# Last feed-forward, first octo: its first product looks two weight tiles ahead instead of four

## The chip, the core and the metric

The kernel runs on one core of a Trainium2 chip. The core has five engines with instruction streams of their own, each worked off in order: TensorE (PE; PEld is its weight load), VectorE (DVE), ScalarE (ACT), GpSimd (POOL) and SyncE (SP), which here only starts transfers. Engines wait for each other on semaphores alone. The metric is the device time of one execution in microseconds (us); lower is better. Times inside a profile count from the start of its span.

## The reference

One layer of a decoder on 512 tokens of width 1024, in float32: a half-step SwiGLU feed-forward, a token mixer (a gated linear recurrence beside sliding-window attention), and a second half-step SwiGLU feed-forward. Each has an RMS norm ahead of it and one behind it. The change lies in the second feed-forward:

```python
def rms_norm(x, g):
    xf = x.astype(jnp.float32)
    y = xf * lax.rsqrt(jnp.mean(xf * xf, axis=-1, keepdims=True) + RMS_EPS)
    return (y * g.astype(jnp.float32)).astype(x.dtype)

def swiglu(x, w_gu, w_down):
    gate, up = jnp.split(x @ w_gu, 2, axis=-1)
    return (jax.nn.silu(gate) * up) @ w_down

    x = x + 0.5 * rms_norm(swiglu(rms_norm(x, ffn2_pre_g[l]), ffn2_w_gu[l], ffn2_w_down[l]), ffn2_post_g[l])
```

The hidden width is 2816, 22 chunks of 128.

## The kernel before

**Split products.** Each float32 operand is split into a rounded high part and the rest. ACT casts the high part (`whi` for weights, `hh` for hidden values), DVE subtracts it to get the low part (`wlo`, `hl`). A product is three matmuls on PE: high by high, high by low, low by high. So each weight tile costs one ACT cast and one DVE subtraction before PE can use it, and PE needs the low part at its second or third matmul.

**Groups of the last feed-forward.** The 22 chunks go in groups (0,6), (6,10), (10,14), (14,18), (18,22). The first group is computed chunk by chunk; its two first chunks go down at once (`classic_down`, results in `yb`). Each of the four others is an "octo": gate and up of four chunks by seven block products instead of eight (method `octo`, L929). Behind each octo come the seven products of the group before it on its way down (`seven_down`, L1083; banks `ya`, `yb`, `yd`, `ye`). The octo with the change is the one of chunks 6 to 9, here "octo 6".

**The seven products of an octo.** Their accumulators are three pairs of PSUM banks, A, D and B (`ab`, `db`, `bb` in the profile). In order: p into A; ACT copies A to B (L953, `each(act.copy, B, A)` at L979); q into D; ACT copies D away; r onto A; s onto B; t onto A; u onto D; v onto A. PE may not start r before the copies of A to B are done, since r goes on accumulating in A.

**The weight tiles of an octo.** Each product uses two weight units, one per half of 512 rows; the profile names them by product and number, such as `whi_bq__6333` and `wlo_bq__6334` for the first q unit and `whi_bq__6337`, `wlo_bq__6338` for the second. Gate and up blocks lie in four raw tiles loaded by SP: `raw_bx__6015`, `raw_bx__6121` (upper rows) and `raw_by__6243`, `raw_by__6246` (lower rows). Some units need a combination of blocks first, made on DVE in place (L294, "pre"): for q and s from the x tile alone, for r from the x tile and the y tile of the same number. Then come the cast on ACT (L283) and the subtraction on DVE (L287).

**What sets the order.** A planner, the class `Weights`, records these instructions when a product takes its unit. `take(ahead)` brings the units up to `ahead` behind the one taken into the streams. While `early` holds, it also rounds one unit more (its pre and its cast) before the low part of the unit at hand. `early` holds when `ahead` is at least `AHEAD`, which is 4:

```python
            if self.rounded == self.split:
                self.round()
            if early and self.rounded == self.split + 1 < len(self.units) and self.units[self.rounded][4]:
                self.round()
            ...
            if early and self.rounded == self.split:
                self.round()
...
        self.fill(1 + ahead, early or ahead >= AHEAD)
```

Whatever is recorded later stands later in its engine's stream. The copies of A to B are recorded behind the two takes of product p and ahead of the takes of product q. There are six buffers each for `whi` and `wlo`, and five for raw tiles.

**Beside the products** the octo also carries the forms for the way down: DVE makes sums of hidden values (`s1` to `s4`), ACT casts them (`hhs`, L824), DVE takes the low parts (`hls`, L831). The fifth product on the way down (bank `ye`) needs the low part of `s4`.

Of the kernel before, what the change touches and what calls it, by code (L numbers as in the profile page):

```python
# [21 lines left out]
FC = F // P  # L22
# [14 lines left out]
AHEAD = 4  # L37
# [84 lines left out]
def tile_layer(ctx: ExitStack, tc: tile.TileContext, out: bass.AP, **ins: bass.AP):  # L122
# [29 lines left out]
    def acc_tile(name):  # L152
        return tmp.tile([P, T], F32, tag="acc", name=name, bufs=3)

    def r_tile(name):
        return big.tile([P, T], F32, tag="R", name=name)

    def wide(name):
        return big.tile([P, NB * T], F32, tag="z", name=name, bufs=2)
# [5 lines left out]
    W = Weights()  # L165
# [630 lines left out]
    class Hidden:  # L796
# [129 lines left out]
            for j in range(2):  # L926
                self.hs[f + j] = hs[j]

        def octo(self, f, beside, soon=False):  # L929


            n = f"{self.name}{f}"

            def did(i):
                for fn in beside.get(i, ()):
                    fn()

            h_hbm = hbm.tile([4 * P, T], F32, name=f"h_{n}")

            def seven(b, form, first, i):  # L940
                for q in range(2):
                    hi, lo = W.take(3 if soon and i == 6 and q else AHEAD)
                    for tb in range(2):
                        blk = slice(tb * P, (tb + 1) * P)
                        for k in range(2):
                            xh, xl = self.nxt.t[form, 2 * q + k]
                            for j, (x, w) in enumerate(((xh, hi), (xl, hi), (xh, lo))):
                                pe.matmul(b[tb], x[:, blk], w[:, k, :], start=first and q + k + j == 0, stop=q + k == 2 and j == 2, skip_group_check=True)  # L948
                    did(i + q / 2)

            def each(fn, *args):
                for xs in zip(*args):
                    fn(*xs)  # L953

            def turned(xs, h):

                for tb, x in enumerate(xs):
                    dve.transpose(z.rearrange("p (j b n) -> p b j n", n=32, b=NB)[:, 2 * h + tb], x.rearrange("p (j n) -> p j n", n=32))

                def put():  # L960
                    for i in range(4):
                        sync.dma_start(h_hbm[:, i * P:(i + 1) * P].rearrange("(j a) n -> a j n", a=32), z[32 * i:32 * (i + 1)].rearrange("p (j n) -> p j n", n=P))

                if h:
                    W.later(1, put)

            def pair(make, name):
                return [make(f"{name}{n}{tb}") for tb in range(2)]

            z = wide(f"z{n}")  # L970
            A, Dd, B = (pair(bank, s) for s in "adb")
            p1, p7, u4 = (pair(wt, s) for s in ("p1", "p7", "u4"))
            u2 = pair(acc_tile, "u2")
            g1 = [acc_tile(f"g1{n}0"), r_tile(f"g1{n}1")]
            silu = lambda o, x: act.activation(o, x, AF.Silu)
            add = lambda o, x: dve.tensor_add(o, o, x)
            mul = lambda o, x: dve.tensor_mul(o, o, x)
            seven(A, "b11", True, 0)
            each(act.copy, B, A)  # L979
            seven(Dd, "t3", True, 1)  # L980
            each(act.copy, p7, Dd)
            seven(A, "t2", False, 2)
            each(act.copy, u2, A)
            seven(B, "b21", False, 3)
            W.later(1, each, silu, p1, B)
            seven(A, "t1", False, 4)
            each(act.copy, u4, A)
            W.later(1, each, add, u4, p7)
            seven(Dd, "t4", False, 5)
            each(add, u2, Dd)  # L990
            each(mul, u2, p1)
            W.later(1, turned, u2, 0)
            seven(A, "b22", False, 6)
            each(silu, g1, A)
            if soon:
                each(mul, g1, u4)
                turned(g1, 1)
            else:
                W.later(1, each, mul, g1, u4)
                W.later(1, turned, g1, 1)  # L1000
            return h_hbm

        def seven_forms_of(self, f, h_hbm, at=(1, 2.5, 3.5, 4.5, 5.5, 6)):

            x = {}

            def fetch():
                if h_hbm is None:
                    z = self.all_held.rearrange("p (s j t) -> p s j t", s=2, j=2)
                    for i in range(2):  # L1010
                        for h in range(2):
                            x[i, h] = z[:, i, :, HALF[h]]
                    return
                z = wide(f"hx{self.name}{f}")
                for s in range(2):
                    for h in range(2):
                        x[s, h] = z[:, (2 * s + h) * T:(2 * s + h + 1) * T]
                        sync.dma_start(x[s, h].rearrange("p (j n) -> p j n", j=2), h_hbm[2 * s * P:2 * (s + 1) * P, HALF[h]].rearrange("(j p) n -> p j n", p=P))

            def begin():  # L1020
                self.forms, self.blocks = {}, {}
                self.seven_left(f, x[0, 0], 0)

            first, second = ([lambda: self.seven_right(f, x[0, 1], 0)], [lambda: self.seven_left(f, x[1, 0], 1)]), [lambda: self.seven_right(f, x[1, 1], 1)]
            step = [lambda: self.steps.pop(0)()]
            return dict(zip(at, ([fetch], [begin], first[0], first[1], second, step)))

        def fetched(self, f, h_hbm, new=t2k):

# [53 lines left out]
    def seven_down(hid, f, one, part, forms, ahead, beside={}, keep=False):  # L1083

        free = [r_tile] + 3 * [acc_tile]
        for fn in beside.get(-1, ()):
            fn()
        A, B, Dd, E_ = ([bank(f"y{s}{hid.name}{f}{i}") for i in range(2)] for s in "abde")  # L1090
        for n, (banks, form, blocks) in enumerate(((A, "a11", []), (Dd, "s3", [(1, 1)]), (B, "a12", [(0, 0)]), (A, "s2", [(1, 0)]),
                                    (E_, "s4", [(0, 1)]), (Dd, "a22", [(1, 0)]), (A, "s1", [(1, 1), (0, 1)]))):
            one(banks, W.take(ahead if form == "a11" else AHEAD), forms[form], form in ("a11", "s3", "s4"))
            if form == "a11":
                for i in range(2):
                    act.copy(B[i], A[i])
            if hid.steps:
                hid.steps.pop(0)()
            for i in range(2 if form in (("s3", "s2") if keep else ("a12", "s3", "s2", "s4", "a22", "s1")) else 0):
                if keep:  # L1100
                    o = part(*blocks[0], i)
                    dve.tensor_add(o, o, banks[i])
                    continue
                st = free.pop()("stage") if free else t2k("stage")
                act.copy(st, banks[i])  # L1105
                for half, dh in blocks:
                    o = part(half, dh, i)
                    pool.dma_start(o, st.rearrange("p (a b) -> p a b", a=2) if len(o.shape) == 3 else st, accum_op=ALU.add)  # L1108
            for fn in beside.get(n, ()):
                fn()  # L1110
        return {(0, 0): B, (1, 0): Dd, (0, 1): E_, (1, 1): A}
# [212 lines left out]
    hid = Hidden("a", n1)  # L1324
# [28 lines left out]
    late, h_hbm, decay = [], {}, []  # L1353
    for g, (f0, f1) in enumerate(GROUPS1):
        if g:
# [5 lines left out]
            before = f0  # L1361
# [472 lines left out]
    hid = Hidden("b", n2)  # L1834
# [46 lines left out]
    h_hbm = {}  # L1881
# [26 lines left out]
    down = lambda half, dh, i: parts[2 * half + i, dh]  # L1908
    for g, (f0, f1) in enumerate(GROUPS2):
        if g:  # L1910
            h_hbm[f0] = hid.octo(f0, hid.seven_forms_of(before, h_hbm[before], (1, 2.5, 3.5, 4.5, 5.5, 6)), f1 == FC)
            kept = seven_down(hid, before, by_tokens, down, hid.forms, AHEAD - 1, *((last, True) if f1 == FC else ()))
            before = f0
            continue
        hid.all_held = wide("u0")
        spare.extend(fours("hs0", F32R))
        held = {f: hid.all_held[:, (f - 2) * T:(f - 1) * T] for f in range(2, f1)}
        h_hbm[2] = None
        turns = [(turn_back, c) for c in range(KD)]
        hs = hid.classic(f1, banks, {2: [(n2.sums, 0)], 2.5: [(n2.lows, 0)] + turns[:2], 3: turns[2:4], 3.5: [(n2.sums, 1)], 4: [(n2.lows, 1)] + turns[4:6], 4.5: [(n2.sums, 2)], 5: [(n2.lows, 2)] + turns[6:], 5.5: [(n2.sums, 3)]}, AHEAD - 1, held)  # L1920

        def others(dh, f):
            for fn, k in {(0, 0): [(n2.lows, 3)]}.get((dh, f), ()):
                fn(k)
            if (dh, f) == (0, 0):
                W.load(2)

        classic_down(hs, f0, 2, others)
        before = 2
# [88 lines left out]
```

## Time and profile before

| | |
|---|---|
| median of 3 runs | 846.49 us (846.41 to 846.69) |
| the profiled execution | 847.31 us, of which its span is 845.6 us |
| PE busy in the span | 835.3 us (99%), 4568 matmuls |
| DVE busy | 734.1 us (87%) |
| ACT busy | 525.1 us (62%) |
| POOL busy | 202.1 us (24%) |
| mean granted TensorE clock | 0.999 |
| octo 6 on PE | from 585.93 us to 625.8 us of the span |

A row of the timeline reads: start, duration, engine, line, operation, output<-inputs, shape, and in brackets the idle time of the engine before it with what ended it. A row of the waits reads: who waited, for whom, us in total, how often, longest. A matmul's duration is longer than its distance to the next one, because matmuls overlap; the same holds for instructions on DVE and ACT, where the next one starts some 0.1 us before the end of the one ahead.

### The profile page before, as it was taken

What the parts mean: (1) busy time and instruction counts of PE and PEld (TensorE: products, weight loads), DVE (VectorE), ACT (ScalarE), POOL (GpSimd) and SP (SyncE); (2) the same over time, 40 slices, a digit from 0 to 9 for tenths busy, and PEclk for the clock granted to TensorE, in tenths of its full rate; (3) what the DMA queues carried; (4) which work ended last, traced back from release to release, by engine and by line L of the source; (5) the groups of instructions that cost most, each with busy time, mean ns of one, the idle gap of its engine ahead of it and who ended that gap; (6) DMA issues with size and microseconds to landing.
All of it is one profiled execution on the core that took longest, in us unless ns stands there. A gap on an engine that the chain in (4) does not pass through costs nothing.

```text
span 845.6 us, 12586 instructions
## 1 busy us (share of the span) xinstructions
PE 835.3 (99%) x4568; PEld 725.1 (86%) x4568; DVE 734.1 (87%) x1020; ACT 525.1 (62%) x875; POOL 202.1 (24%) x213
## 2 busy tenths in 40 slices
PE   9999999999999999999999999999999999999996
PEld 9988888988988998998788899888788888888885
DVE  4978999988979865889989589799998998998996
ACT  6746756676666655556888447436657767666562
POOL 2023000230320334334456055112004114032001
PEclk9999999999999999999999999999999999999999
DMA  7249419397594899231311130167639939769742
GB/s 250 76 141 348 158 47 320 84 246 251 140 253 169 178 274 322 74 101 50 101 50 51 50 121 31 50 167 190 231 110 230 319 89 250 256 152 259 297 138 101
DMA packets 122767, 142.18 MB, mean 168 GB/s; under 512 B 23680, under 2 KB 81360, under 8 KB 122192
## 3 DMA queue, kind: packets, MB, share of 16 engines
q1 hardware_dynamic: 108576, 110.81, 40.8%
q0 software_dynamic: 13984, 30.42, 16.8%
q8 instruction: 36, 0.59, 0.3%
q14 instruction: 27, 0.22, 0.1%
q10 hardware_dynamic: 144, 0.13, 0.0%
HBM read 100.45 MB, written 40.89 MB: 167 GB/s over the span
## 4 chain that ended last, share of the span: by engine, by line
PE 89%; DVE 5%; DMA 2%; ACT 2%; issue 1%; POOL 1%; SPq 0%; DVEq 0%; ACTq 0%; POOLq 0%
PE aa L948 10%; PE ab L948 10%; PE da L948 5%; PE db L948 5%; PE yaa L1339 3%; PE bb L948 3%; PE ba L948 3%; PE yda L1339 2%; PE ya L498 2%; PE ya L499 2%; PE ya L500 2%; PE aa L878 1%; PE a_first L1198 1%; PE yab L1865 1%; PE yab L1863 1%; PE yab L1864 1%
## 5 line engine op out<-in xcount | busy, mean ns | idle before, releaser
L1108 POOL DMA_DIRECT2D yp_a<-stage x42 | 36.8, 1067 | 181.7 <-ACT stage L1105 160.9
L1108 POOL DMA_DIRECT2D yp_b<-stage x42 | 36.3, 1032 | 144.9 <-ACT stage L1105 121.6
L498 PE MATMUL ya<-hha,whi_ad 128*128 128x512 f32 x62 | 24.1, 389 | 0.0
L499 PE MATMUL ya<-hla,whi_ad 128*128 128x512 f32 x62 | 24.1, 389 | 0.0
L500 PE MATMUL ya<-hha,wlo_ad 128*128 128x512 f32 x62 | 24.1, 389 | 0.0
L681 POOL TENSOR_TENSOR acca_r<-acca_r,sq_r 128x512 f32<-128x512 f32 x6 | 8.0, 1326 | 45.4 <-ACT sq_r L529 45.4
L1977 POOL TENSOR_TENSOR last<-yp,grow 128x512 f32<-128x512 f32 x3 | 3.9, 1293 | 58.3 <-DVE yp L1972 58.3
L517 PE MATMUL an<-xh_mx,whi_xl 128*128 128x256 f32 x64 | 15.8, 287 | 0.0
L518 PE MATMUL an<-xh_mx,wlo_xl 128*128 128x256 f32 x64 | 15.5, 283 | 0.0
L1973 ACT ACTIVATE ysq<-yp 128x512 f32<-128x512 f32 (+1 forms) x9 | 5.3, 585 | 15.9 <-DVE yp L1972 15.7
L498 PE MATMUL gt<-xh_mx,whi_gt 128*128 128x512 f32 x32 | 14.2, 444 | 0.0
L500 PEld LDWEIGHTS ya<-hha,wlo_ad 128*128 128x128 f32 x62 | 11.6, 188 | 2.4
L1105 ACT COPY stage<-yab 128x512 f32<-128x512 f32 x12 | 6.5, 601 | 11.6 <-DMA yp_b<-stage 11.6
L498 PEld LDWEIGHTS ya<-hha,whi_ad 128*128 128x128 f32 x62 | 11.6, 188 | 2.4
L499 PEld LDWEIGHTS ya<-hla,whi_ad 128*128 128x128 f32 x62 | 11.6, 188 | 2.4
L529 ACT ACTIVATE sq_r<-yp_a 128x256 f32<-128x256 f32 (+1 forms) x10 | 5.0, 502 | 12.4 <-DVE yp_a L671 5.3
L498 PE MATMUL pub<-xh_f,whi_bu 128*128 128x512 f32 x32 | 12.6, 395 | 0.0
L500 PE MATMUL gt<-xh_mx,wlo_gt 128*128 128x512 f32 x32 | 12.6, 394 | 0.0
L498 PE MATMUL pgb<-xh_f,whi_bg 128*128 128x512 f32 x32 | 12.6, 393 | 0.0
L499 PE MATMUL gt<-xl_mx,whi_gt 128*128 128x512 f32 x32 | 12.6, 392 | 0.0
L498 PE MATMUL pq<-xh_mx,whi_q 128*128 128x512 f32 x32 | 12.5, 392 | 0.0
L573 ACT ACTIVATE xh_f<-xT,cols 128x256 fp32r<-128x256 f32 x16 | 8.1, 508 | 7.0 <-DVE xT L712 6.4
(2021 smaller groups left out, 3531.4 us busy)
## 6 DMA issues: line engine op xcount, KB each, us to landing
yp_a<-stage POOLq DMA_DIRECT2D x50, 256.0 KB, 8.9
yp_b<-stage POOLq DMA_DIRECT2D x50, 256.0 KB, 10.1
h_a<-za SPq DMA_DIRECT2D x16, 256.0 KB, 4.5
hxa<-h_a SPq DMA_DIRECT2D x16, 256.0 KB, 17.9
h_b<-zb SPq DMA_DIRECT2D x16, 256.0 KB, 3.7
hxb<-h_b SPq DMA_DIRECT2D x16, 256.0 KB, 18.8
xn<-in_x SPq DMA_DIRECT2D x8, 256.0 KB, 4.6
xT_hbm<-xT POOLq DMA_DIRECT2D x2, 1024.0 KB, 9.6
```

Of the source, the lines that this page charges most:

```text
L498: pe.matmul(ps, hi[:, k, :], xh, start=start, stop=False)
L499: pe.matmul(ps, hi[:, k, :], xl, start=False, stop=False)
L500: pe.matmul(ps, lo[:, k, :], xh, start=False, stop=stop)
L517: pe.matmul(ps[:, sl], hi[:, k, :], xh, start=k == 0, stop=False)
L518: pe.matmul(ps[:, sl], lo[:, k, :], xh, start=False, stop=False)
L878: pe.matmul(o, w[:, k, js], x, start=first and i + j + k == 0, stop=k == 3 and i == 2, skip_group_check=True)
L948: pe.matmul(b[tb], x[:, blk], w[:, k, :], start=first and q + k + j == 0, stop=q + k == 2 and j == 2, skip_group_check=True)
L1108: pool.dma_start(o, st.rearrange("p (a b) -> p a b", a=2) if len(o.shape) == 3 else st, accum_op=ALU.add)
L1198: pe.matmul(banks[j][:, HALF[0]], ws[j][part][:, k, :], n1.xs[k][xpart][:, HALF[0]], start=k == 0 and part == xpart, stop=stop and k == KD ...
L1339: pe.matmul(o, a[:, k, ms], x[:, js], start=first and i + k + m % 2 == 0, stop=k == 1 and i == 2, skip_group_check=True)
L1863: pe.matmul(banks[i], hh[:, js], hi[:, k, :], start=first and k == 0, stop=False, skip_group_check=True)
L1864: pe.matmul(banks[i], hh[:, js], lo[:, k, :], start=False, stop=False, skip_group_check=True)
```

## The change

Octo 6 takes the two units of its first product (p) with `ahead` 2 instead of 4; all other takes, and all other octos, keep 4. Because 2 is below `AHEAD`, `early` is off for these two takes as well, so within them a unit's pre and cast are recorded behind the low part of the unit ahead. A second edit gives `seven_forms_of` one more `step` at the end of its tuple; the places `at` have six entries and the tuple is cut to them, so it adds nothing.

```diff
-        def octo(self, f, beside, soon=False):
+        def octo(self, f, beside, soon=False, lead=AHEAD):
...
-                    hi, lo = W.take(3 if soon and i == 6 and q else AHEAD)
+                    hi, lo = W.take(3 if soon and i == 6 and q else lead if i < 1 else AHEAD)
...
-            return dict(zip(at, ([fetch], [begin], first[0], first[1], second, step)))
+            return dict(zip(at, ([fetch], [begin], first[0], first[1], second, step, step)))
...
-            h_hbm[f0] = hid.octo(f0, hid.seven_forms_of(before, h_hbm[before], (1, 2.5, 3.5, 4.5, 5.5, 6)), f1 == FC)
+            h_hbm[f0] = hid.octo(f0, hid.seven_forms_of(before, h_hbm[before], (1, 2.5, 3.5, 4.5, 5.5, 6)), f1 == FC, 2 if g == 1 else AHEAD)
```

No instruction is added or removed. The streams of POOL and SP are the same, and so is PE's order. Two streams change, both between the last casts ahead of product q and those of product s.

ACT's stream in octo 6, before: the casts of both q units, both r units and the first s unit (L283), and only then the two copies of A to B.

```order
L283 CAST whi_bq6__6333<-raw_bx60__6015 128x1024
L283 CAST whi_bq6__6337<-raw_bx61__6121 128x1024
L283 CAST whi_br6__6342<-raw_bx60__6015 128x1024
L283 CAST whi_br6__6347<-raw_bx61__6121 128x1024
L283 CAST whi_bs6__6364<-raw_by60__6243 128x1024
L953 COPY bb60_6320<-ab60_6316 128x512
L953 COPY bb61_6321<-ab61_6317 128x512
L283 CAST whi_bs6__6383<-raw_by61__6246 128x1024
```

The same place of ACT's stream, after (lines from 930 on stand one lower, and the buffers of the same units have other numbers):

```order
L283 CAST whi_bq6__6333<-raw_bx60__6015 128x1024
L283 CAST whi_bq6__6350<-raw_bx61__6121 128x1024
L954 COPY bb60_6320<-ab60_6316 128x512
L954 COPY bb61_6321<-ab61_6317 128x512
L283 CAST whi_br6__6369<-raw_bx60__6015 128x1024
L283 CAST whi_br6__6373<-raw_bx61__6121 128x1024
L283 CAST whi_bs6__6378<-raw_by60__6243 128x1024
L283 CAST whi_bs6__6383<-raw_by61__6246 128x1024
```

The two copies have moved ahead of three casts, the two of r and the first of s.

DVE's stream at the same place, before: pre of q for both x tiles, then the low part of the first q unit, the pre of r for the first x tile, the low part of the second q unit, and the pre of r that reads the raw tile `by61`.

```order
L294 TENSOR_TENSOR raw_bx60__6015<-raw_bx60__6015 128x2x512
L294 TENSOR_TENSOR raw_bx61__6121<-raw_bx61__6121 128x2x512
L287 TENSOR_TENSOR wlo_bq6__6334<-raw_bx60__6015,whi_bq6__6333 128x1024
L294 TENSOR_TENSOR raw_bx60__6015<-raw_by60__6243,raw_bx60__6015 128x2x512
L287 TENSOR_TENSOR wlo_bq6__6338<-raw_bx61__6121,whi_bq6__6337 128x1024
L294 TENSOR_TENSOR raw_bx61__6121<-raw_by61__6246,raw_bx61__6121 128x2x512
L287 TENSOR_TENSOR wlo_br6__6343<-raw_bx60__6015,whi_br6__6342 128x1024
```

The same place of DVE's stream, after:

```order
L294 TENSOR_TENSOR raw_bx60__6015<-raw_bx60__6015 128x2x512
L287 TENSOR_TENSOR wlo_bq6__6334<-raw_bx60__6015,whi_bq6__6333 128x1024
L294 TENSOR_TENSOR raw_bx61__6121<-raw_bx61__6121 128x2x512
L287 TENSOR_TENSOR wlo_bq6__6351<-raw_bx61__6121,whi_bq6__6350 128x1024
L294 TENSOR_TENSOR raw_bx60__6015<-raw_by60__6243,raw_bx60__6015 128x2x512
L294 TENSOR_TENSOR raw_bx61__6121<-raw_by61__6246,raw_bx61__6121 128x2x512
L287 TENSOR_TENSOR wlo_br6__6370<-raw_bx60__6015,whi_br6__6369 128x1024
```

The same instructions stand in another order: each low part of q now follows at once on the pre of its own unit, and the pre of r for the first x tile has moved behind both low parts of q.

## The prediction

> **What bounds the kernel now.** I read the page first: busy times, then the chain that ended last.
>
> ```profile
> span 845.6 us, 12586 instructions
> PE 835.3 (99%) x4568; PEld 725.1 (86%) x4568; DVE 734.1 (87%) x1020; ACT 525.1 (62%) x875; POOL 202.1 (24%) x213
> PE 89%; DVE 5%; DMA 2%; ACT 2%; issue 1%; POOL 1%; SPq 0%; DVEq 0%; ACTq 0%; POOLq 0%
> ```
>
> PE is busy nearly always and carries 89% of the chain, so the time changes only where PE comes to wait more or less. The waits of PE alone are the next view (who <- whom, line: total us, times, longest).
>
> ```profile
> PE ab L948 <- ACT bb L953: 1.3, 1, 1.3
> PE yeb L1865 <- DVE hls L831: 0.3, 1, 0.3
> ```
>
> Of the whole last feed-forward these two are PE's only waits. The first is the one that the change aims at: product r of octo 6 waits for the copies of A to B. The second comes 39 us later, on the way down. PE's timeline at the first:
>
> ```profile
> 594.54 0.39 PE L948 MATMUL db<-wlo_bq__6338,t13h_f 128*128 128x512 f32 x1
> 596.58 0.39 PE L948 MATMUL db<-wlo_bq__6338,t13h_f 128*128 128x512 f32 x1
> 598.24 0.50 PE L948 MATMUL ab<-whi_br__6342,t24h_f 128*128 128x512 f32 x1 [1.27 <-ACT bb L953]
> 598.57 0.39 PE L948 MATMUL ab<-whi_br__6342,t24l_f 128*128 128x512 f32 x1
> 598.80 0.40 PE L948 MATMUL ab<-wlo_br__6343,t24h_f 128*128 128x512 f32 x1
> 603.83 0.39 PE L948 MATMUL bb<-whi_bs__6364,b2h_f 128*128 128x512 f32 x1
> ```
>
> From 594.54 to 596.58 lie nine steps, so a matmul takes 0.227 us. Product r was due at 596.81 and starts at 598.24. Product s, due 24 matmuls (5.44 us) behind 596.81, at 602.25, starts at 603.83: the wait costs PE 1.58 us in all, restart included.
>
> ACT's timeline shows why the copies are late.
>
> ```profile
> 588.53 1.11 ACT L283 CAST whi_bq__6333<-raw_bx__6015 128x1024 fp32r<-128x1024 f32 x1
> 589.66 1.06 ACT L283 CAST whi_bq__6337<-raw_bx__6121 128x1024 fp32r<-128x1024 f32 x1
> 592.24 1.06 ACT L283 CAST whi_br__6342<-raw_bx__6015 128x1024 fp32r<-128x1024 f32 x1 [1.52 <-DVE raw_bx__6015 L294]
> 595.71 1.05 ACT L283 CAST whi_br__6347<-raw_bx__6121 128x1024 fp32r<-128x1024 f32 x1 [2.41 <-DVE raw_bx__6121 L294]
> 596.66 1.04 ACT L283 CAST whi_bs__6364<-raw_by__6243 128x1024 fp32r<-128x1024 f32 x1
> 597.61 1.06 ACT L953 COPY bb<-ab 128x512 f32<-128x512 f32 x2
> ```
>
> The second r cast waits 2.41 us for a DVE combination, and the copies stand behind it although A was finished long before. DVE over the same stretch:
>
> ```profile
> 587.27 1.22 DVE L294 TENSOR_TENSOR raw_bx__6015<-raw_bx__6015 128x1024 f32<-128x1024 f32 x1
> 588.41 1.22 DVE L294 TENSOR_TENSOR raw_bx__6121<-raw_bx__6121 128x1024 f32<-128x1024 f32 x1
> 589.67 1.23 DVE L287 TENSOR_TENSOR wlo_bq__6334<-raw_bx__6015,whi_bq__6333 128x1024 fp32r<-128x1024 f32 x1
> 590.93 1.23 DVE L294 TENSOR_TENSOR raw_bx__6015<-raw_by__6243,raw_bx__6015 128x1024 f32<-128x1024 f32 x1
> 592.07 1.22 DVE L287 TENSOR_TENSOR wlo_bq__6338<-raw_bx__6121,whi_bq__6337 128x1024 fp32r<-128x1024 f32 x1
> 594.39 1.23 DVE L294 TENSOR_TENSOR raw_bx__6121<-raw_by__6246,raw_bx__6121 128x1024 f32<-128x1024 f32 x1 [1.10 <-DMA raw_by__6246<-in_ffn_w_gu]
> 595.53 1.22 DVE L287 TENSOR_TENSOR wlo_br__6343<-raw_bx__6015,whi_br__6342 128x1024 fp32r<-128x1024 f32 x1
> ```
>
> DVE in turn waited 1.10 us for the raw tile `by61` to land. The last view is DVE from there to PE's second wait, first as sums over stretches (length, busy time per engine with counts, clock, DMA share, GB/s), then the rows at that wait.
>
> ```profile
> 594.40:637.40 43.00, 41.44 (x183) 33.65 (x181) 41.67 (x47) 27.60 (x40) 0.21 (x1) 1.00 0.46 159
> 590.00:594.40 4.40, 4.40 (x21) 3.65 (x20) 3.26 (x4) 1.78 (x2) 0.00 (x0) 1.00 1.03 389
> 611.38 0.69 DVE L831 TENSOR_TENSOR hls<-s3b,hhs 128x512 fp32r<-128x512 f32 x1 [0.69 <-ACT hhs L824]
> 635.50 1.23 DVE L320 TENSOR_TENSOR wlo_bdu__6672<-raw_byd__6442,whi_bdu__6671 128x1024 fp32r<-128x1024 f32 x1 [0.50 <-ACT whi_bdu__6671 L316]
> 636.64 0.68 DVE L831 TENSOR_TENSOR hls<-s4b,hhs 128x512 fp32r<-128x512 f32 x1
> 636.69 0.39 PE L1864 MATMUL yeb<-wlo_bdt__6622,hhs 128*128 128x512 f32 x1
> 637.38 0.50 PE L1865 MATMUL yeb<-whi_bdt__6621,hls 128*128 128x512 f32 x1 [0.29 <-DVE hls L831]
> ```
>
> DVE is busy 41.67 of 43.00 us (third number behind the length). Its two gaps, 0.69 and 0.50 us, are round trips: DVE makes a sum, ACT casts it, DVE goes on. Nothing in these 43 us lets DVE catch up, and PE at 637.38 waits for its `hls`. So this stretch has two chains that meet there: PE's, and DVE's, which starts from 594.39. DVE's is the longer one, by 0.46 us (PE was due at 636.69 + 0.23 = 636.92).
>
> **The change part by part.** The extra `step`, the `lead` argument and the shift by a line put nothing into a stream: nothing.
>
> *The copies ahead of three casts.* They now stand behind the second q cast. Product q begins 14 matmuls ahead of 594.54, at 591.4, and A's last matmul, one step ahead of that and 0.39 long, ends at 591.5. So the copies will run as soon as ACT comes to them, by my sum below at 593.1 to 594.1, 2.7 us before r is due at 596.81. The wait of 1.58 us is gone. For the casts behind them, see the next step.
>
> *DVE's new order.* Before, the second pre of q filled the time in which ACT cast the first q unit. Now DVE goes pre, wait for the cast, low part, twice over. From the rows: first pre ends 588.49, cast 588.53 to 589.64, first low part 589.67 as before, so DVE idles 1.18 us that it worked before. The second pre starts 1.14 us later (start to start of two such rows, 595.53 − 594.39), 590.81, and ends at 592.03. ACT follows 0.04 to 0.08 us behind (588.49 to 588.53; 592.16 to 592.24) and takes 1.06: until 593.15. The second low part of q runs 593.18 to 594.41; PE wants it at 594.54, a margin of 0.13. DVE has idled 1.15 us more. Then the pre of r for the first x tile at 594.32, that for the second at 595.46; `by61` is there since 594.35, so the 1.10 us wait is gone. The first r cast runs 595.63 to 596.69, and the low part of r starts at 596.72 instead of 595.53.
>
> So DVE gains back 1.10 us and loses 1.18 + 1.15 us, and is about 1.2 us late from there. All its later instructions stand in the old order, with both round trips, which shift with it.
>
> *What PE does with it.* Product r starts in time at 596.81, but its third matmul wants the low part at 597.26 and gets it at 596.72 + 1.22 = 597.94, a new wait of 0.7 us. Compared with 598.80 before, PE is still 0.86 us ahead. The later low parts arrive in time: the second of r stands two places behind the first, starts 2 × 1.14 behind 596.72 and ends at 600.2, and PE reaches it 12 matmuls behind 597.94, at 600.7. PE carries the 0.86 us on to the way down, is due there at 636.06, and finds `hls`, which ended at 637.32, ending at 638.52. The gain is given back and 1.2 us are added: PE goes on at 638.57 instead of 637.38.
>
> *Behind it.* PE has no wait between 637.4 and the end, so nothing there can take the delay up; DVE has idle time again only later.
>
> ```profile
> 653.59 1.22 DVE L287 TENSOR_TENSOR wlo_br__6844<-raw_bx__6523,whi_br__6843 128x1024 fp32r<-128x1024 f32 x1 [2.33 <-ACT whi_br__6843 L283]
> 637.40:840.00 202.60, 201.25 (x898) 167.00 (x898) 183.87 (x215) 128.38 (x191) 40.01 (x45) 1.00 0.77 212
> ```
>
> Transfers that SP starts when DVE frees a raw tile move with DVE by the same 1.2 us. **Sum:** −1.58 at r, +0.7 at r's low part, and a wait at `ye` that grows from 0.5 to 2.5 us; the net is DVE's delay, +1.2 us. The profiled execution took 847.31 us, 0.82 above the median of 846.49; I put the sum on both, 848.5 for a profiled one and 847.7 for the median.
>
> **What is unknown** is when `by61` lands without the profiler. Were it there earlier, the kernel before would already run faster in the plain runs than its profile shows, and the loss would be larger. Before, DVE could have used it from 592.07 + 1.22 = 593.29, so at most 1.10 us more: +2.3. Were it later, by up to 1.1, the loss shrinks towards 0. In the 4.4 us ahead of its landing the transfers moved 389 GB/s with all 16 DMA engines busy (share 1.03), and nothing in that queue is changed; I keep the profile's time.
>
> The Trainium skill, page "DMA: Bandwidth & Descriptors", section "Where 436 GB/s comes from", puts a ceiling of 435.2 GB/s on a core's 16 ports. As an estimate from that page, at that rate the 4.4 us would shrink to 3.9, so landing 0.5 us earlier and +1.7 instead of +1.2; the row's 389 GB/s lies below the ceiling, and no run here shows the transfer alone.
>
> **The rivals.**
>
> *The wait is simply gone.* PE keeps the 1.58 us: 844.9. That needs `hls` of `s4` no later than 637.32 − 1.1. Against it speak the wait row that names `hls` and the 41.67 busy of 43.00 us. Chance 0.04.
>
> The Trainium skill, "Perfetto Trace Analysis", section "Optimization Strategy", advises to find the gaps of the engine that matters, see which semaphore ends them, and make that dependency start or finish sooner. By it alone this edit is right and gives 844.9; the trace agrees on the first gap and shows the second behind it.
>
> *Given back exactly.* The casts overlap more than I count, or `by61` lands late, so DVE reaches r's low part within 0.4 us of before. Then PE's saved time only lengthens its wait at `ye`: 846.5, up to 846.9. For it: 1.10 of DVE's 2.3 us are already covered by a wait. Against: the round trip of pre, cast and low part is read directly from rows. Chance 0.14.
>
> *Slower beyond 0.2%.* `by61` lands at least 0.5 us earlier in plain runs, before 593.85, and the kernel before loses nothing to it: +1.7 to +2.3, 848.2 to 848.8. For it: the profiled execution is 0.82 us longer than the median, and part of that may be transfers slowed by profiling. Against: those 0.82 us may as well lie at start and end. Chance 0.19.
>
> *The change does nothing* because the copies were waiting for PE rather than for the casts: excluded by the ACT rows, which run cast to copy without a gap.
>
> **How the numbers follow.** My forecast, DVE 0.4 to 1.7 us late, has 0.63: 847.7. The rivals have 0.04, 0.14 and 0.19. A difference of 0.2%, 1.69 us, is about what a measurement of this kernel can tell from no change. The first rival ends just inside that bound, so I give 0.03 to faster; slower is the third rival with a little of the forecast's upper edge, 0.21; the rest, 0.76, is within. The range takes in both the exact return and the early landing: 846.4 to 848.8.
>
> **What the profile after would show.** Right: the wait of `ab` for `bb` is gone; DVE idles about 1.2 us before each low part of q, for ACT; the first low part of r starts near 596.7; PE waits some 2 us for `hls` at `ye`, restarting near 638.5; span 846.8. Wrong: if PE passes `ye` near 637.4 or earlier, DVE was not late; if PE has a new wait for the second low part of q (margin 0.13 us), the first margin was too thin, without effect on the end.

## The result, and the profile after

| | before | after |
|---|---|---|
| median of 11 executions each | 846.64 us (846.21 to 848.50) | 849.89 us (848.40 to 850.34) |
| ratio after to before | | 1.0029 (95% interval 1.0021 to 1.0037) |
| the profiled execution, and its span | 847.31, 845.6 us | 849.95, 848.2 us |
| mean granted clock in it | 0.999 | 0.995 |

The changed kernel is slower, by about 0.3%, and its median lies above the range given. The page's totals have grown by the loss, and the share of DVE in the chain that ended last has gone from 5% to 9%:

```profile
span 848.2 us, 12582 instructions
PE 837.4 (99%) x4568; PEld 726.2 (86%) x4568; DVE 734.3 (87%) x1020; ACT 525.2 (62%) x875; POOL 201.9 (24%) x213
PE 85%; DVE 9%; issue 2%; ACT 2%; POOL 1%; DMA 1%; DVEq 0%; ACTq 0%; POOLq 0%
```

PE's waits of the changed kernel (who <- whom: total us, times, longest). The wait for the copies to `bb` is gone; two others stand in its place:

```profile
PE yeb L1866 <- DVE hls L831: 1.8, 1, 1.8
PE ab L949 <- DVE wlo_br__6370 L287: 0.4, 1, 0.4
```

DVE's timeline, over product q and at the low part of `s4`. The first two rows carry the round trips (DVE makes a sum, ACT casts it, DVE goes on), 1.18 and 1.12 us of idling, and the sum for r that takes `by61` (595.49) no longer waits:

```profile
589.74 1.23 DVE L287 TENSOR_TENSOR wlo_bq__6334<-raw_bx__6015,whi_bq__6333 128x1024 fp32r<-128x1024 f32 x1 [1.18 <-ACT whi_bq__6333 L283]
593.22 1.23 DVE L287 TENSOR_TENSOR wlo_bq__6351<-raw_bx__6121,whi_bq__6350 128x1024 fp32r<-128x1024 f32 x1 [1.12 <-ACT whi_bq__6350 L283]
595.49 1.22 DVE L294 TENSOR_TENSOR raw_bx__6121<-raw_by__6246,raw_bx__6121 128x1024 f32<-128x1024 f32 x1
596.70 1.22 DVE L287 TENSOR_TENSOR wlo_br__6370<-raw_bx__6015,whi_br__6369 128x1024 fp32r<-128x1024 f32 x1
637.82 0.68 DVE L831 TENSOR_TENSOR hls<-s4b,hhs 128x512 fp32r<-128x512 f32 x1
```

ACT's timeline: the copies run at 593.09, directly behind the second q cast, where they ran at 597.61 before.

```profile
592.13 1.05 ACT L283 CAST whi_bq__6350<-raw_bx__6121 128x1024 fp32r<-128x1024 f32 x1 [2.43 <-DVE raw_bx__6121 L294]
593.09 1.07 ACT L954 COPY bb<-ab 128x512 f32<-128x512 f32 x2
595.61 1.06 ACT L283 CAST whi_br__6369<-raw_bx__6015 128x1024 fp32r<-128x1024 f32 x1 [1.46 <-DVE raw_bx__6015 L294]
```

PE's timeline at product r and at `ye`. Product r starts at 596.90 instead of 598.24; at `ye` PE stands from 636.7 to 638.56.

```profile
596.90 0.40 PE L949 MATMUL ab<-whi_br__6369,t24h_f 128*128 128x512 f32 x1
597.98 0.51 PE L949 MATMUL ab<-wlo_br__6370,t24h_f 128*128 128x512 f32 x1 [0.44 <-DVE wlo_br__6370 L287]
636.23 0.49 PE L1865 MATMUL yeb<-wlo_bdt__6622,hhs 128*128 128x512 f32 x1
638.56 0.80 PE L1866 MATMUL yeb<-whi_bdt__6621,hls 128*128 128x512 f32 x1 [1.84 <-DVE hls L831]
639.16 0.63 PE L1864 MATMUL yeb<-whi_bdt__6621,hhs 128*128 128x512 f32 x1
641.72 0.52 PE L1864 MATMUL yeb<-whi_bdt__6621,hhs 128*128 128x512 f32 x1
642.08 0.39 PE L1865 MATMUL yeb<-wlo_bdt__6622,hhs 128*128 128x512 f32 x1
```

Up to 638.56 this is the forecast to within a few hundredths of a microsecond (638.57). Then something comes that it did not have. From 638.56 to 642.08 PE does eight steps in 3.52 us; at the usual 0.227 us they take 1.82, so 1.7 us are lost with nothing to wait for. The view by stretches names the cause (length, busy time of PE, PEld, DVE, ACT and POOL with counts, granted clock, DMA share, GB/s):

```profile
636.00:638.00 2.00, 0.73 (x2) 0.19 (x1) 1.50 (x3) 2.00 (x4) 0.00 (x0) 1.00 0.81 191
638.00:640.00 2.00, 1.44 (x3) 1.16 (x4) 2.00 (x3) 2.00 (x5) 1.63 (x2) 0.64 1.17 266
640.00:642.00 2.00, 2.00 (x6) 1.60 (x5) 2.00 (x4) 2.00 (x4) 1.46 (x3) 0.50 0.76 108
```

The granted clock is 0.50 there. So the span is 638.56 − 637.38 = 1.2 us longer up to `ye`, and 1.4 us longer behind it: PE makes up some 0.2 to 0.3 us of the 1.7 later; these views do not show where.

### The profile page after: what moved, and what is told of

It reads as the page before. It is cut to its first block, busy times and chain, and to the rows that moved or that the text cites. A ratio compares the mean times of both kernels' runs of the same rounds, so it can differ in the third digit from the quotient of the medians.

```text
span 848.2 us, 12582 instructions
## 1 busy us (share of the span) xinstructions
PE 837.4 (99%) x4568; PEld 726.2 (86%) x4568; DVE 734.3 (87%) x1020; ACT 525.2 (62%) x875; POOL 201.9 (24%) x213
## 4 chain that ended last, share of the span: by engine, by line
PE 85%; DVE 9%; issue 2%; ACT 2%; POOL 1%; DMA 1%; DVEq 0%; ACTq 0%; POOLq 0%
PE aa L949 10%; PE ab L949 8%; PE da L949 5%; PE db L949 4%; PE yaa L1340 3%; PE ba L949 3%; PE yda L1340 2%; PE bb L949 2%; PE ya L498 2%; PE ya L499 2%; PE ya L500 2%; PE a_first L1199 1%; PE aa L878 1%; PE wo L1795 1%; PE yab L1866 1%
## 5 line engine op out<-in xcount | busy, mean ns | idle before, releaser
L500 PE MATMUL pgb<-xh_f,wlo_bg 128*128 128x512 f32 x32 | 12.5, 390 | 0.0
L499 PE MATMUL pq<-xl_mx,whi_q 128*128 128x512 f32 x32 | 12.5, 390 | 0.0
```

Source lines behind the costliest of these rows:

```text
L499: pe.matmul(ps, hi[:, k, :], xl, start=False, stop=False)
L500: pe.matmul(ps, lo[:, k, :], xh, start=False, stop=stop)
```

## The experiments

Three theories were open. First: DVE's two round trips cost about 2.2 us, and the first profile of the kernel before hid half of that, because there DVE also waited 1.10 us for `by61`. Second: the half clock behind the new gap at `ye` is a part of the price. Third: it is not DVE's order but the copies, which now run ahead of r's casts on ACT. The expectations below number them otherwise: their theory 1 is a DVE 1.2 us late with the half clock behind it, their theory 2 is `by61` landing earlier in plain runs, and their theory 3 is the copies.

To compare profiles, the table at the end of the next part counts from the start of DVE's last low part of product p (`wlo_bp__6172`), because the same instruction starts between 585.85 and 587.69 us in these profiles.

### How long DVE is late: both kernels profiled again

Both kernels without an edit, one profile each, twice.

> The kernel before once more, one look. The first profile of it had DVE waiting 1.10 us for the raw tile by61 and a span of 845.6 us. Theory 1 with the landing as a part of it: the landing differs between executions, and whatever DVE waits for by61 here shows in the span, 844.5 us plus that wait (0 to 1.1), if the first 60 us are undisturbed. If the landing does not matter, the span does not go with that wait.

> The changed kernel once more, one look. Theory 1: DVE reaches the first low part of r 1.15 to 1.2 us behind what the order of before needs with by61's wait in it, hls of s4 ends near 638.5 us and PE has a gap of 1.8 us at ye; the span is 848.2 if the clock row behind the gap shows half speed again, 846.7 if it does not. Theory 2: the span is 848 or more with full clock as well.

> The kernel before, a third look. 49.4 us plus the wait for by61 from the last low part of p to the low part of s4; the wait between 0 and 1.1 us.

> The changed kernel, a third look. 51.6 us from the last low part of p to the low part of s4, whatever the execution, and a gap of 1.8 us on PE at ye; behind it either full clock, or half speed for 3.4 us and a span 1.5 us longer.

Single times: 847.07 and 848.98 us, then 847.18 and 849.39 us. DVE's and PE's timelines of the kernel before in the second of these profiles (before_look2):

```profile
593.02 1.22 DVE L287 TENSOR_TENSOR wlo_bq__6338<-raw_bx__6121,whi_bq__6337 128x1024 fp32r<-128x1024 f32 x1
594.27 1.23 DVE L294 TENSOR_TENSOR raw_bx__6121<-raw_by__6246,raw_bx__6121 128x1024 f32<-128x1024 f32 x1
595.42 1.22 DVE L287 TENSOR_TENSOR wlo_br__6343<-raw_bx__6015,whi_br__6342 128x1024 fp32r<-128x1024 f32 x1
598.13 0.50 PE L948 MATMUL ab<-whi_br__6342,t24h_f 128*128 128x512 f32 x1 [0.66 <-ACT bb L953]
637.26 0.50 PE L1865 MATMUL yeb<-whi_bdt__6621,hls 128*128 128x512 f32 x1 [0.31 <-DVE hls L831]
```

The row at 594.27 has no bracket: DVE did not wait for `by61`. With that the wait of PE for the copies was only 0.66 us, half of the first profile's. before_look reads the same (0.63 us for the copies, none for `by61`). Its span of 845.3 us is not the 844.5 expected without that wait, because `wlo_bp` itself starts 0.75 us later than in the first profile; counted from there, the expectation holds (49.4 us). The changed kernel in after_look2, PE's timeline at `ye`:

```profile
639.57 0.50 PE L1866 MATMUL yeb<-whi_bdt__6621,hls 128*128 128x512 f32 x1 [1.83 <-DVE hls L831]
640.37 0.39 PE L1866 MATMUL yeb<-whi_bdt__6621,hls 128*128 128x512 f32 x1
641.06 0.39 PE L1866 MATMUL yeb<-whi_bdt__6621,hls 128*128 128x512 f32 x1
```

Same gap, full clock: three steps in 0.69 us. In after_look the clock stays at 1.00 behind the same gap, too, with a span of 847.3 us.

### The landing of `by61`, moved on purpose

How long `by61` takes from its issue to its landing is in the view of the transfers (how many, KB each, median us to landing), here of the kernel before in its first profile and of lead2_early, which has the same order on DVE:

```profile
raw_by__6246<-in_ffn_w_gu SPq DMA_DIRECT2D x2, 512.0 KB, 9.8
raw_by__6246<-in_ffn_w_gu SPq DMA_DIRECT2D x2, 512.0 KB, 7.6
```

Over the 14 profiles of this case without an extra transfer it takes 6.9 to 10.1 us, issued always 1.6 to 2.2 us ahead of the start of `wlo_bp`, and lands 4.8 to 8.3 us behind the start of `wlo_bp`. DVE's old order can use it 7.15 us behind that start (593.29 − 586.14 in the first profile). Four of the 14 land later than that, and the first profile of the kernel before, with 8.2, is one of them.

To move the landing, in both kernels SP makes one more transfer ahead of `by61`, a strip of 128 x 1024 weights into scratch memory of which nothing is used.

```diff
+        if name == "by61_":
+            sync.dma_start(hbm.tile([P, D], F32, name="extra"), ins["ffn2_w_gu"][0, :P, :D])
```

> The kernel before, with one extra transfer of 512 KB, from HBM to HBM, that SP starts just ahead of the load of the raw tile by61; nothing reads it. It makes by61 land later by 1 to 3 us. Theory (by61's landing decides how much the change costs): DVE waits for by61 by more than 1.1 us, and the time from the last low part of p to the low part of s4 (49.4 us without that wait, 50.5 with 1.10 of it) grows by the same amount, to 51.5 or more; the span goes with it, beside what the first 60 us add.

> The changed kernel with the same extra transfer. Theory: DVE needs by61 1.15 to 2.2 us later than the kernel before does, so it waits less for it, and the two kernels come together: from the last low part of p to the low part of s4 it takes the same time as in the kernel before with the extra transfer, within 0.2 us, where without it they lay 1.1 (by61 late) or 2.2 us (by61 early) apart. If by61 has nothing to do with it, the changed kernel stays 1.1 to 2.2 us behind.

Single times: 849.02 and 849.30 us, beside 847.04 for the kernel before. DVE's timeline of the kernel before with the late tile:

```profile
596.38 1.23 DVE L296 TENSOR_TENSOR raw_bx__6121<-raw_by__6246,raw_bx__6121 128x1024 f32<-128x1024 f32 x1 [3.24 <-DMA raw_by__6246<-in_ffn_w_gu]
638.62 0.69 DVE L833 TENSOR_TENSOR hls<-s4b,hhs 128x512 fp32r<-128x512 f32 x1
```

and of the changed kernel:

```profile
596.60 1.23 DVE L296 TENSOR_TENSOR raw_bx__6121<-raw_by__6246,raw_bx__6121 128x1024 f32<-128x1024 f32 x1 [0.43 <-DMA raw_by__6246<-in_ffn_w_gu]
638.84 0.69 DVE L833 TENSOR_TENSOR hls<-s4b,hhs 128x512 fp32r<-128x512 f32 x1
```

Once both wait for the tile, they run alike from there: 42.24 us from that sum to `hls` in both, and 847.3 and 847.6 us of span. That stretch takes 42.2 to 42.4 us in every profile that leaves `hls` in its place, so what differs between them is made ahead of that sum. The agreement counted from `wlo_bp` is worse than I had expected, 52.63 against 52.04 us in the table instead of within 0.2, because DVE's own start differs by 0.81 us between these two profiles while the landing differs by 0.22. What follows: the price of DVE's new order is set by how late `by61` lands. Late, the order costs nothing; early, it costs nearly the whole of the two round trips (2.16 of 2.30 us, below).

The readings together, in us. "To `hls`" runs from the start of `wlo_bp__6172` to the start of the low part of `s4`, "to the end" from the same start to the end of the span, which is taken to 0.1 us. The clock is that of the 10 us behind the restart at `ye`.

| kernel | DVE's wait for `by61` | to `hls` | to the end | lowest clock close behind `ye` |
|---|---|---|---|---|
| before, first profile | 1.10 | 50.50 | 259.46 | 1.00 |
| before, two later profiles | 0 | 49.44, 49.43 | 258.41, 258.41 | 1.00 |
| after, first profile | 0 | 51.61 | 261.99 | 0.50 |
| after, two later profiles | 0 | 51.61, 51.60 | 260.43, 260.37 | 1.00 |
| before, late `by61` | 3.24 | 52.63 | 261.31 | 1.00 |
| after, late `by61` | 0.43 | 52.04 | 260.80 | 1.00 |

The changed kernel needs 51.6 us to `hls` every time that it does not wait for `by61`. The kernel before needs 50.5 or 49.4, by the landing. So the loss is 51.60 − 49.44 = 2.16 us at `hls` and 260.40 − 258.41 = 2.0 us at the end: the first theory. The half clock adds 261.99 − 260.40 = 1.6 us where it comes.

### Does the half clock come often enough to count?

The changed kernel, and the same kernel with eight matmuls of no use in the gap. They write the bank `ye`, and the product that follows starts that bank afresh.

```diff
+            if form == "s4" and hid.name == "b" and f == 2:
+                for _ in range(8):
+                    pe.matmul(E_[0], forms["s2"][0][:, :P], w[0][:, 0, :], start=True, stop=True, skip_group_check=True)
...
```

> The changed kernel, with eight extra matmuls on PE between the fourth and the fifth product of the way down behind octo 6. They write the bank ye before its product starts, which overwrites them, so they only keep PE busy for 8 x 0.227 = 1.8 us in the gap where it waits for hls of s4. Theory 1 (the end is set by DVE's delay of 1.2 us, and the gap of 2.3 us on PE lowers its clock to half for one stretch, another 1.5 us): the clock stays at 1.00 behind the gap, PE still restarts at ye near 638.5 us, the span is 846.7 to 846.9 instead of 848.2, and the plain times lose their upper group near 850. Theory 2 (the loss beyond 1.2 us comes from the raw tile by61 landing earlier in plain runs, the slow matmuls cost nothing): the times stay at 848.4 to 850.3 and the profile's end moves by less than 0.3 us.

filled8 took 849.45 us (848.63 to 849.83, six executions), 1.0031 (1.0019 to 1.0042) of the kernel before, at clocks of 0.997 and 0.998. So 0.3% was lost with no half clock behind the gap, and the span of 846.7 to 846.9 us that theory 1 expected did not come (848.1). But its profiled execution had also lost 0.6 us in the kernel's first part, to a wait (`a_first` for `xh_a`) that most other profiles show at 0.2 us or not at all, and to the end it needed 260.41 us, as much as the changed kernel's later profiles. One series did not separate the two theories. Two more, on one chip, did better:

> The changed kernel unedited, eleven executions beside those of the kernel before. If the half clock behind the gap of 1.83 us at `ye` is part of the change's price, these executions fall into two groups again: some with a mean clock of 0.995 to 0.996 and a span about 1.6 us above the others (848.2 to 848.6 against 846.7 to 847.2 before), between a third and two thirds of them, and the median ratio is 1.0025 to 1.004. If it was chance of that chip, all clocks are 0.997 or more, spans 846.5 to 848.3 by how the start went, and the ratio is 1.002 to 1.003: DVE's loss of 2.0 us alone is 1.0024.

> The changed kernel with eight matmuls of no use in the gap at `ye`, on the same chip as after_again. The gap is 0.4 us here, so if the gap brings the half clock, no execution is below 0.997 while some of after_again are, and the median lies below after_again's by the share of fallen executions: 0.3 to 1.5 us. If the clock falls for another reason, as many executions of this one have 0.995 to 0.996. If it falls in neither, both medians agree within 0.4 us, both about 2.0 us above the kernel before.

| | executions | median us | ratio to before (95%) | clock of the executions |
|---|---|---|---|---|
| after_again | 5 | 850.14 | 1.0036 (1.0023 to 1.0048) | 0.996, 0.996, 0.997, 0.998, 0.995 |
| filled8_again | 11 | 848.97 | 1.0022 (1.0013 to 1.0031) | 0.997 to 0.999 |
| before, beside both | 15 | 847.22 | | 0.997 to 0.999 |

The profile of after_again, PE's timeline and the stretches behind the gap:

```profile
639.90 0.50 PE L1866 MATMUL yeb<-whi_bdt__6621,hls 128*128 128x512 f32 x1 [1.83 <-DVE hls L831]
640.47 0.50 PE L1865 MATMUL yeb<-wlo_bdt__6622,hhs 128*128 128x512 f32 x1
640.77 0.63 PE L1866 MATMUL yeb<-whi_bdt__6621,hls 128*128 128x512 f32 x1
644.11 0.39 PE L1865 MATMUL ydb<-wlo_bdu__6672,hha 128*128 128x512 f32 x1
```

```profile
638.00:640.00 2.00, 0.17 (x2) 0.11 (x1) 1.99 (x3) 2.00 (x4) 0.29 (x1) 1.00 0.88 220
640.00:642.00 2.00, 2.00 (x6) 1.58 (x7) 2.00 (x3) 2.00 (x4) 1.85 (x3) 0.65 1.21 201
642.00:644.00 2.00, 2.00 (x6) 1.58 (x5) 2.00 (x3) 1.74 (x3) 1.61 (x3) 0.50 0.79 213
```

And of filled8_again, where the filling leaves 0.38 us of the gap:

```profile
637.00 1.98 PE L1096 MATMUL yeb<-whi_bds__6594,hhs 128*128 128x512 f32 x8
639.81 0.50 PE L1870 MATMUL yeb<-whi_bdt__6621,hls 128*128 128x512 f32 x1 [0.38 <-DVE hls L831]
640.15 0.40 PE L1868 MATMUL yeb<-whi_bdt__6621,hhs 128*128 128x512 f32 x1
```

The intervals of the two ratios overlap, but four of the five executions of after_again took longer than the longest of filled8_again, 849.63 us. The mean clock tells which executions had the half clock: every profile has half clock in its last 1.7 to 5.1 us as well, which alone makes means of 0.997 to 0.999, and a half clock of 3.4 us behind the gap takes off another 0.002. Over all series, 8 of the 18 executions of the unedited changed kernel have a mean clock of 0.996 or less, and none of the 17 with the gap filled, which start `ye` no later. So the half clock is tied to the gap, and it counts. In the first series the five executions at 0.995 and 0.996 average 850.13 us and the six others 848.82, against 846.64 before: +3.5 and +2.2. The median falls among the upper ones. The second theory holds beside the first: about 2 us are DVE's, in every execution, and some 1.2 to 1.6 us more come in nearly half of them (1.2 between the two groups of after_again, 1.6 between the profiles). One execution in each series is as slow at a clock of 0.998 (849.98 and 850.02 us), for a reason that is not known.

### Which part of the change costs: DVE's order or ACT's

Two kernels do one half of the change each. lead2_early keeps `ahead` at 2 for product p but lets the early rounding on, so DVE's stream is the old one and only the copies stand earlier. copies_late adds a fill ahead of the copies, so ACT's stream is the old one and DVE's the new. Set beside each other, the streams of the profiles have just these orders.

```diff
# lead2_early
-                    hi, lo = W.take(3 if soon and i == 6 and q else lead if i < 1 else AHEAD)
+                    hi, lo = W.take(3 if soon and i == 6 and q else lead if i < 1 else AHEAD, i < 1 and lead < AHEAD)
# copies_late
             seven(A, "b11", True, 0)
+            if lead < AHEAD:
+                W.fill(4, True)
             each(act.copy, B, A)
```

> Lead 2 for the first product of octo 6, but with early rounding kept on: DVE's order is that of the kernel before, and the copies of A to B move ahead of two casts only (second of r, first of s). Theory 1: the wait for the copies is gone, DVE is not late, hls of s4 ends at 637.3 as before, PE restarts at ye at 637.4, and the gap there grows from 0.5 to 2.0 us. Span 845.6 if the clock holds through that gap, 847 if it falls. Theory 3 (the copies' place on ACT is what costs time, by the casts that they delay): DVE late by 1 us as in the changed kernel, span 846.7 or more.

> DVE's order of the changed kernel with ACT's order of the kernel before: the copies stand behind both casts of r and the first of s again. Theory 1: DVE is late by 1.2 us all the same, hls of s4 ends at 638.5 and PE restarts at ye near 638.55; the copies run at 598.7 to 599.7, so product r starts at 599.2 and the gap ahead of it is 2.3 us, start to start beyond a matmul's own time. Span 846.8 if the clock holds through that gap, about 848.3 if it falls there. Theory 3: with the copies back the time of before returns, 845.6 for the span.

lead2_early: 846.65 us (845.97 to 848.27, 11 executions), 1.0000 (0.9991 to 1.0009). copies_late: 849.29 us (848.53 to 849.96, six), 1.0031 (1.0019 to 1.0043). The kernel before had 846.92 beside them. PE's only wait in the last feed-forward and DVE's `hls` in lead2_early, from the waits and the timeline:

```profile
PE yeb L1866 <- DVE hls L831: 1.2, 1, 1.2
```

```profile
635.76 0.69 DVE L831 TENSOR_TENSOR hls<-s4b,hhs 128x512 fp32r<-128x512 f32 x1
```

It starts `hls` 49.44 us behind `wlo_bp`, exactly as the kernel before. PE no longer waits at r and waits 1.2 us at `ye` instead of 0.3: the gain is given back there, and the time does not change. (The 2.0 us expected at `ye` came from a sum with the first profile's wait for `by61`.) Two of PE's waits (a third, at product q, is 0.2 us) and DVE's first low part of r in copies_late:

```profile
PE ab L949 <- ACT bb L954: 2.3, 1, 2.3
PE yeb L1868 <- DVE hls L831: 0.5, 1, 0.5
```

```profile
597.37 1.23 DVE L287 TENSOR_TENSOR wlo_br__6368<-raw_bx__6015,whi_br__6367 128x1024 fp32r<-128x1024 f32 x1
```

It reaches `hls` in 51.66 us, as the changed kernel, with the copies late. Its span of 847.5 us is longer than the 846.8 expected because `wlo_bp` starts 0.6 us later than in the changed kernel's first profile. So DVE's order alone is the loss, the copies alone are no gain, and the third theory falls.

### Taking away the bound at `ye`

If DVE's chain to `hls` sets the end, then making that low part earlier must gain, in either kernel. Here the planner fills ahead and takes the step that issues `hls` before product `s3` instead of behind it, so `hls` stands ahead of the low part `wlo_bdu` on DVE.

```diff
+            ahead_of = form == "s3" and hid.name == "b" and f == 2
+            if ahead_of:
+                W.fill(4, True)
+                hid.steps.pop(0)()
             one(banks, W.take(ahead if form == "a11" else AHEAD), forms[form], form in ("a11", "s3", "s4"))
...
-            if hid.steps:
+            if hid.steps and not ahead_of:
                 hid.steps.pop(0)()
```

before_s4 is the kernel before with this edit, after_s4 the changed kernel with it, and both is lead2_early with it.

> The kernel before with only the move of the low part of s4. Theory 1: the first wait of PE (for the copies, 1.4 us) stays, the second (0.5 us) goes: span 0.5 to 0.6 us below before, 844.9 against 845.6 with by61's wait, or 844.0 against 844.5 without.

> The changed kernel, and on the way down behind octo 6 DVE takes the low part of s4 ahead of that of weight unit u. The low parts of weights are as late as in the changed kernel. Theory 1: hls of s4 ends at 636.8 instead of 638.5, PE restarts at ye at 636.85, its gap is 0.8 us or less, the clock never falls; span 845.2, 1.5 us below the changed kernel's undisturbed 846.7, and no upper group of times near 850. If DVE's delay itself, at whatever instruction, sets the end, a later product waits in its place and the span stays at 846.7.

> Lead 2 with early rounding on, and on the way down behind octo 6 DVE takes the low part of s4 ahead of the low part of weight unit u instead of behind it. Theory 1: hls of s4 ends at 635.6 instead of 637.3, PE's gap at ye is 0.3 us or less, the 1.58 us of the first wait are kept and most of the 0.59 us of the second as well: span 843.6 to 844.0, time 844.6 to 845.2. If DVE's work as a whole sets the end and not this one low part, a new wait stands a product later at yd or ya, and the span stays above 844.6.

| | median us | ratio to before (95%) | to `hls` | to the end |
|---|---|---|---|---|
| before_s4 | 846.02 (845.51 to 846.88), 11 executions | 0.9985 (0.9976 to 0.9994) | 48.08 | 257.99 |
| after_s4 | 847.64 (847.25 to 848.93), 11 | 1.0007 (0.9998 to 1.0015) | 49.87 | 259.72 |
| both | 845.72 (845.15 to 848.05), 11 | 0.9988 (0.9980 to 0.9997) | 47.72 | 257.55 |

In before_s4 PE has no wait at `ye` any more; its waits and DVE's row:

```profile
PE ab L948 <- ACT bb L953: 0.6, 1, 0.6
```

```profile
634.09 0.67 DVE L831 TENSOR_TENSOR hls<-s4b,hhs 128x512 fp32r<-128x512 f32 x1
636.08 0.39 PE L1869 MATMUL yeb<-whi_bdt__6621,hls 128*128 128x512 f32 x1
```

That is 0.15% faster than the kernel before, which is little, but its interval lies below 1. In after_s4 `hls` comes 1.74 us earlier than in the changed kernel, yet only 260.40 − 259.72 = 0.7 us are left at the end. The rest is lost one octo later, where PE meets the same low part again, which this edit leaves in its place:

```profile
694.91 0.50 PE L1870 MATMUL yeb<-whi_bdt__7122,hls 128*128 128x512 f32 x1 [0.52 <-DVE hls L831]
```

The matmul ahead of it starts at 694.00, so 0.91 − 0.23 = 0.7 us of the lost microsecond go there. Beside after_look2, and counted from `wlo_bp`, PE is ahead by 1.73 us at the first `ye`, by 1.54 just ahead of this wait and by 0.86 behind it; what takes the small rest is not shown. The kernel both likewise keeps a wait for later copies, in the next octo, so adding the early copies to before_s4 brings nothing that these runs can tell, and its median lies 0.5 us above the 844.6 to 845.2 expected:

```profile
654.02 0.50 PE L949 MATMUL ab<-whi_br__6800,t24h_f 128*128 128x512 f32 x1 [0.45 <-ACT bb L954]
```

## Why the prediction was wrong

- **The copies and PE's wait for them**: right. Copies at 593.09 (593.1 forecast), the wait gone.
- **DVE's two round trips**: right. Idle 1.18 and 1.12 us (1.18 and 1.15), first low part of r at 596.70 (596.72). The margin of 0.13 us at the second low part of q was too thin, without effect on the end: PE slipped there by 0.2 us.
- **PE's new wait and the meeting at `ye`**: right. The third matmul of r starts at 597.98 (597.94), PE goes on at `ye` at 638.56 (638.57). That the saved wait is given back is shown apart from DVE's delay by lead2_early, where `hls` starts 49.44 us behind `wlo_bp` as before and the ratio is 1.0000. The changed kernel's own timeline needed no guess about `by61`.
- **"So DVE gains back 1.10 us"**: this is the step that failed, with the sentence behind it, "I keep the profile's time". The 1.10 us was what one execution showed. Four later profiles with DVE's old order (before_look, before_look2, lead2_early, both) have no wait for `by61` at all, and before_s4 has 0.39 us. Without the term DVE is 2.16 us late instead of 1.2. That is the third rival's mechanism, to which I gave 0.19, and the pair with the late tile shows that the landing decides. My reason for that rival, transfers slowed by profiling, is not what the runs show: the later executions were profiled as well. It is the landing that varies between executions, with 6.9 to 10.1 us from issue to landing. That the first two profiles differ by the forecast 1.2 us at `ye` does not confirm the term: the forecast and this difference start from the same execution of the kernel before.
- **"PE has no wait between 637.4 and the end, so nothing there can take the delay up"**: true of waits, but it left out what a gap does to the clock. No term of the sum and no rival had a fall of the granted clock. In the first profile it cost 1.6 us, in nearly half the executions about 1.2 to 1.6, and it lifts the median from what filled8_again gives, 846.64 x 1.0022 = 848.5 us, inside the range, to 849.89, outside it.
- **The sign**: within 0.2% had 0.76 and slower 0.21. Both misses push to the slow side: 2.0 us is 0.24%, and the clock makes it 0.29%.

## What to carry to other kernels

A wait that one profile shows on a DMA is a poor thing to subtract: ask what the sum is with it and without it, and look at a second execution before one end is chosen. Where an engine waits early and again later for another chain, the later meeting decides; bring that chain to the meeting earlier, as before_s4 did by moving one low part ahead of another. And a wait moved to one place and grown to 1.83 us cost TensorE its clock behind the gap in a part of the executions; waits of 0.3 to 1.3 us did not in any profile here.

## What was not expected of the hardware

**The clock fell behind a gap of 1.83 us, but not always.** The half clock lasted 3.4 us each time (638.6 to 642.0, and 640.6 to 644.0, where PE had first run 0.7 us at full clock). By the mean clock it came in at least 8 of 18 executions with this gap. In the clock records of all 16 profiles the changes are whole multiples of 3.413 us apart: after has 185 of them at full clock, one at half and 59 at full, the kernel before 245 at full. So each trace shows where such windows of 3.413 us lie, and how the longest gaps lie in them:

| profile, place | PE's gap | its parts in the windows | half clock |
|---|---|---|---|
| after, `ye` | 1.84 | 1.84 | from 638.57, the window's end |
| after_again, `ye` | 1.83 | 1.83 | from 640.60, the window's end |
| after_look, `ye` | 1.83 | 1.83 | none |
| after_look2, `ye` | 1.83 | 0.93, 0.90 | none |
| after_late61, `ye` | 1.84 | 1.53, 0.31 | none |
| before_late61, product r | 3.36 | 1.71, 1.65 | none |
| copies_late, product r | 2.27 | 0.80, 1.47 | none |

Both falls have the whole gap in one window and begin at that window's end. None of the gaps that a window's end cuts brought one, not even that of 3.36 us. But after_look has its whole gap in one window, 0.06 us behind its start, and kept its clock, so what else decides stays open. The six executions of copies_late, at 0.997 or more, do not show that its gap never brings the half clock: a fall in an execution whose half clock at the end is short would read 0.997 as well.

The Trainium skill, page "TensorE: Matmul & The Clock Gate", section "What's actually happening", lets the clock drop to half behind at least one idle window of about 3.4 us, and has this window run freely, so that it depends on the execution where in it a gap lies. The length of the half clock, the grid and its coming in some executions only agree with that; a fall behind 1.83 us of idling does not follow from it.

**The same tile takes 6.9 to 10.1 us to land.** That is the time of `by61` from issue to landing in the 14 profiles without an extra transfer; these runs do not show why it varies. In the first profile DVE could take it at 594.39 us of the span; in lead2_early and both, DVE took it at 593.51 and 593.04 without waiting, and in before_s4 at 593.56 after waiting 0.39 us.
